# Attention scores of a head across two PSUM banks, one mask-and-maximum instruction per head

## Chip, cores and metric

One core of one Trainium2 chip. The metric is the device time of one execution in microseconds (us); of several runs the median is given. TensorE is PE here, VectorE DVE, ScalarE ACT, GpSimd POOL; SP issues the DMAs.

## What is computed (reference, cut)

One decoder layer on 1024 tokens with 1024 channels, all float32: an input projection, native sparse attention (8 heads of 64, in two groups of 4) beside a gated DeltaNet, an output projection, and a SwiGLU block. The change touches the attention alone. Each query attends three ways, with a softmax of its own each time, and gates mix the results:

```
p_cmp: softmax over 63 compressed keys            (mask: block ends before the query)
idx  : top 8 of 16 blocks of 64 keys by the summed p_cmp (first, own and previous block forced)
o_slc: softmax over the keys of the chosen blocks (causal)
o_win: softmax over the last 512 keys             (causal)
o_nsa = gate0 * o_cmp + gate1 * o_slc + gate2 * o_win
```

## The kernel before

The program is written for a framework that orders each engine's instructions itself, by its own estimates, and sets the semaphores; buffers come from pools with a fixed number per tag. PSUM has 8 banks of 512 float32 per partition.

The attention stage lies between about 470 and 780 us of the span. It walks over 16 units (i, g): i is a block of 128 queries, g a group of 4 heads. For each unit `merge` (L1129) interleaves three generators by weight: `scores` of the next unit, `values` of this one, and as filler `wob` (L1111), the half of the output projection that belongs to the DeltaNet.

`scores` (L917) has two phases of four heads each.

- Local phase. Two matmuls (L941, high and low part of the keys) give the 128 own-block scores and the 64 compressed ones, 192 columns, two heads in one bank; two more (L949) give the up to 512 earlier window scores into another bank. DVE masks the 64 (L942), the earlier window scores (L951) and the own block (L955), and takes the minimum of each piece on the way (an accumulator read follows each such instruction); L955 continues the minimum that L951 found. ACT takes the exponentials (L944, L957) and sums them.
- Then for i of 4 and more the top-8 choice on DVE (L967 to L978), which gives `bm`, one mask value per block of 64 keys.
- Selected phase. The scores of i + 1 blocks of keys (L997) go in pieces of at most 512 into one bank each; DVE masks each piece (L1007, with `bm` for i of 4 and more) and the own block (L1011); ACT takes the exponentials (L1014).
- The reciprocal sums are multiplied by the gates on DVE (L962, L1019), and POOL (DVE for i = 0) scales the probabilities by them (`pscale`, L914).

`values` (L1027) turns the scaled probabilities: pair by pair of 128x128 blocks, four transposes on PE (L1063; L1057 for the compressed ones) into a bank of tag b, a rounded copy on ACT (L1065), the rest on DVE (L1066), and three pairs later the products on PE (L1043) into the one bank of tag c, one for each pair of heads. At the end of a pair of heads ACT copies half of c (L1047) and DVE adds the two halves (L1048).

`wob` adds its 512 columns to the residual through ACT (L1124, out of PSUM) and POOL (L1125).

The banks of the stage: a (scores) 3, b (transposes) 3, c (products) 1, mm (filler) 1.

## Time and profile before

| | |
|---|---|
| median of 3 runs | 1513.57 us (1512.15 to 1517.66) |
| the profiled execution | 1515.43 us, of it span 1513.7 us |
| busy in the span: PE, DVE, ACT, POOL | 1436.1, 964.8, 722.9, 727.1 us |
| attention stage, 480 to 780 us: PE, DVE, ACT, POOL | 284.3, 257.6, 241.3, 169.0 us of 300 |

An engine is busy while any of its instructions runs. On DVE an instruction's duration reaches some 0.07 to 0.08 us past the start of the next one, so the distance of two starts is what it takes of the queue. On PE the ends are modelled, and matmuls overlap: four 128x128 transposes start 0.11 us apart though each lasts 0.27.

### The profile page before, as it was taken

To read this page: it belongs to the slowest core of one execution; us is meant where nothing else is said; L and a number is where in the kernel's file an instruction comes from. 1 tells how busy PE (TensorE), PEld (TensorE's weight loads), DVE (VectorE), ACT (ScalarE), POOL (GpSimd) and SP (SyncE) were. 2 spreads that over 40 slices of the span, in tenths; PEclk is the share of its full clock that TensorE was granted. 3 is DMA by queue.
4 is the path that set the end of the run, shared out by engine and by line. 5 is a ranking of instruction groups with operands and counts; after the bars stand their busy time and mean duration, and the time that the engine had idled before them with its cause. 6 is when DMAs were issued, how large, how long until landed. Compare 5 with 4: busy or idle time off the path is not lost.

```text
span 1513.7 us, 23493 instructions
## 1 busy us (share of the span) xinstructions
PE 1436.1 (95%) x8000; PEld 1225.8 (81%) x8000; DVE 964.8 (64%) x2276; ACT 722.9 (48%) x1604; POOL 727.1 (48%) x763
## 2 busy tenths in 40 slices
PE   8889999989899999999999899999999999999997
PEld 7878877889898787878887688888888887888886
DVE  4326688836635798998956565444444444999955
ACT  5433356236544898788765433323333332344423
POOL 1232235520240665554467666666566663345445
PEclk9999999999998999999999899999999999999998
DMA  8822255487535223101037122222222227544003
GB/s 259 285 65 84 90 184 159 112 189 229 172 108 195 92 74 101 50 22 43 30 124 245 32 88 84 84 84 84 84 84 84 84 84 262 195 135 133 1 1 111
DMA packets 142743, 174.96 MB, mean 116 GB/s; under 512 B 26912, under 2 KB 79392, under 8 KB 142496
## 3 DMA queue, kind: packets, MB, share of 16 engines
q1 hardware_dynamic: 142624, 173.47, 36.6%
q8 instruction: 63, 1.03, 0.3%
q14 instruction: 56, 0.46, 0.1%
HBM read 122.01 MB, written 51.41 MB: 115 GB/s over the span
## 4 chain that ended last, share of the span: by engine, by line
PE 61%; DVE 11%; ACT 5%; issue 4%; POOL 3%; DMA 3%; POOLq 0%; SPq 0%; ACTq 0%; DVEq 0%
PE mm L119 16%; PE mm L121 16%; PE mm L120 16%; PE c L1043 3%; PE b L1063 2%; DVE PT L1066 2%; PE a L610 1%; ACT Ps L1014 1%; DVE cy L429 1%; DMA vT<-gD 1%; PE a L997 1%; PE a L617 1%; ACT PT L1065 1%; DVE tmp L574 1%; PE b L625 1%
## 5 line engine op out<-in xcount | busy, mean ns | idle before, releaser
L1200 POOL TENSOR_TENSOR A<-wq,A 128x512 fp32r<-128x512 f32 x94 | 135.2, 1440 | 87.5 <-ACT A L1199 79.1
L1199 ACT ACTIVATE A<-wq 128x512 fp32r<-128x512 f32 x96 | 60.1, 630 | 133.0 <-PE mm L121 116.9
L119 PE MATMUL mm<-w,xh 128*128 128x256 f32 x384 | 111.7, 291 | 11.7 <-ACT kst L827 6.2
L1066 DVE TENSOR_TENSOR PT<-b,PT 128x512 fp32r<-128x512 f32 (+2 forms) x168 | 103.8, 621 | 19.0 <-ACT PT L1065 17.2
L120 PE MATMUL mm<-w,xh 128*128 128x256 f32 x384 | 110.9, 289 | 1.0 <-POOL w L208 1.0
L121 PE MATMUL mm<-w,xl 128*128 128x256 f32 x384 | 110.6, 288 | 0.0
L1065 ACT ACTIVATE PT<-b 128x512 fp32r<-128x512 f32 (+2 forms) x168 | 89.1, 539 | 37.6 <-PE b L1063 31.2
L1200 POOL TENSOR_TENSOR wk<-wq,wk 128x512 fp32r<-128x512 f32 x61 | 81.5, 1338 | 52.9 <-ACT wk L1199 44.3
L1043 PE MATMUL c<-PT,vs 128*128 128x256 f32 x528 | 92.9, 300 | 0.1
L208 POOL TENSOR_TENSOR w<-wraw,w 128x512 fp32r<-128x512 f32 x48 | 63.4, 1337 | 56.8 <-ACT w L205 56.8
L119 PEld LDWEIGHTS mm<-w,xh 128*128 128x128 f32 x384 | 75.0, 195 | 12.4 <-ACT kst L827 6.4
L1199 ACT ACTIVATE wk<-wq 128x512 fp32r<-128x512 f32 x63 | 39.6, 630 | 87.6 <-PE mm L121 79.9
L119 PE MATMUL mm<-T,A 128*128 128x512 f32 x200 | 79.1, 396 | 0.0
L120 PE MATMUL mm<-T,A 128*128 128x512 f32 x200 | 79.1, 396 | 0.0
L121 PE MATMUL mm<-T,A 128*128 128x512 f32 x200 | 79.1, 396 | 0.0
L120 PEld LDWEIGHTS mm<-w,xh 128*128 128x128 f32 x384 | 75.0, 195 | 1.2 <-POOL w L208 1.2
L119 PE MATMUL mm<-xh,w 128*128 128x512 f32 x192 | 75.6, 394 | 0.0
L121 PE MATMUL mm<-xh,w 128*128 128x512 f32 x192 | 75.2, 392 | 0.0
L121 PEld LDWEIGHTS mm<-w,xl 128*128 128x128 f32 x384 | 74.9, 195 | 0.1
L1043 PEld LDWEIGHTS c<-PT,vs 128*128 128x128 f32 x528 | 73.0, 191 | 2.5 <-DVE PT L1066 0.3
L1501 DVE TENSOR_TENSOR B<-B,mm 128x512 f32<-128x512 f32 x100 | 63.4, 677 | 17.9 <-PE mm L121 15.0
L120 PE MATMUL mm<-xl,w 128*128 128x512 f32 x192 | 74.8, 389 | 0.0
(471 smaller groups left out, 4533.0 us busy)
## 6 DMA issues: line engine op xcount, KB each, us to landing
wq<-in_w_gu SPq DMA_DIRECT2D x92, 256.0 KB, 2.7
aD<-ring SPq DMA_DIRECT2D x44, 256.0 KB, 2.2
ring<-aD SPq DMA_DIRECT2D x44, 256.0 KB, 3.9
raw<-in_w_dn SPq DMA_DIRECT2D x36, 256.0 KB, 3.8
qk<-gD SPq DMA_DIRECT2D x16, 512.0 KB, 4.8
wraw<-in_w_out SPq DMA_DIRECT2D x28, 256.0 KB, 2.9
wraw<-in_w_tok SPq DMA_DIRECT2D x24, 256.0 KB, 3.1
wraw<-in_w_gdn SPq DMA_DIRECT2D x24, 256.0 KB, 2.8
```

Of the source, the lines that this page charges most:

```text
L119: mm(ps, lhsT=lh, rhs=rh, start=first, stop=False, skip_group_check=grow)
L120: mm(ps, lhsT=lh, rhs=rl, start=False, stop=False, skip_group_check=grow)
L121: return mm(ps, lhsT=ll, rhs=rh, start=False, stop=last, skip_group_check=grow)
L208: (lo or G).tensor_tensor(out=wt[:, 1, k0:k0 + n, :], in0=raw, in1=f32(wt[:, 0, k0:k0 + n, :]), op=ALU.subtract)
L429: V.scalar_tensor_tensor(out=y, in0=cr[:, j:j + 512], scalar=cw[:, j:j + 1], in1=y, op0=ALU.mult, op1=ALU.add)
L1043: mm(po[:, 0:256], lhsT=v, rhs=PT[0:K, a, b_ * 256:(b_ + 1) * 256], start=(n_ == 0 and a == 0), stop=(last and b_ == len(vs) - 1 and a == 1))
L1063: tpose(pt[:, o_:o_ + P], src[:, hh, b * P:(b + 1) * P], ident)
L1065: act(out=PT[0:K, 0, 0:w], in_=pt[0:K, 0:w], func=AF.Copy)
L1066: V.tensor_tensor(out=PT[0:K, 1, 0:w], in0=pt[0:K, 0:w], in1=f32(PT[0:K, 0, 0:w]), op=ALU.subtract)
L1199: act(out=dst[:, 0], in_=src, func=AF.Copy)
L1200: after(eng.tensor_tensor(out=dst[:, 1], in0=src, in1=f32(dst[:, 0]), op=ALU.subtract), prev)
L1501: V.tensor_tensor(out=out_, in0=a_, in1=b_, op=op)
```

## The change

- Tag a now has 2 buffers of 1024 columns, two adjacent banks each; b has 2 banks in place of 3; c is one bank that lies allocated throughout, its two halves of 256 columns serving the two pairs of heads; mm stays. That is 4 + 2 + 1 + 1 = 8 banks.
- Local phase: the 192 columns stand at 512 to 703, the earlier window scores end at 511, so the 640 window columns are adjacent over the bank edge. One instruction masks them all (L944 of the changed kernel) from one joint mask `winm`.
- Selected phase: the two pieces lie on either side of the bank edge, and one instruction masks a head's whole row. For i below 4 it uses `winm`; for i of 4 and more it uses `bm` for all blocks, and the causal mask of the own block is added by PE: one more matmul per head (L993), identity by the causal matrix, into the same bank.
- The gates are the second scalar of the scaling, so L962 and L1019 fall away; so does a multiplication in the top-8 choice (L973).
- `wob` adds to the residual on DVE straight from PSUM (L1102); the ACT copy and the POOL addition fall away.

```diff
...
-    add("caus", np.where(c <= r, 0.0, NEG))
-    add("far", np.concatenate([np.where(c > r, 0.0, NEG), np.zeros((P, 384))], 1))
+    add("winm", np.concatenate([np.where(c > r, 0.0, NEG), np.zeros((P, 384)), np.where(c <= r, 0.0, NEG)], 1))
...
+    V.tensor_copy(causr, C("winm")[:, 512:640])
...
     def bank(tag):
-        return mk(pps3, [P, 512], tag, F32, {"mm": 1, "a": 3, "b": 3, "c": 1}[tag])
+        return mk(pps3, [P, 1024 if tag == "a" else 512], tag, F32, {"mm": 1, "a": 2, "b": 2}[tag])
+
+    pvs = mk(pps3, [P, 2, 256], "c", F32)
...
-    def pscale(i, ap, sc, k):
-        (V if i < EARLY[k] else G).tensor_scalar(ap, ap, sc, 1.0, op0=ALU.mult, op1=ALU.mult)
+    def pscale(i, ap, sc, gt, k):
+        (V if i < EARLY[k] else G).tensor_scalar(ap, ap, sc, gt, op0=ALU.mult, op1=ALU.mult)
...
-            if hh == 0:
-                s2 = bank("a")
-            o = hh * 192
+
+            s1 = bank("a")
+            w0_ = 512 - np_ * P
             for a in range(2):
-                mm(s2[:, o:o + 192], lhsT=QS[:, h, :], rhs=KSw[a][:, g, i, :], start=(a == 0), stop=(a == 1))
-            V.tensor_tensor_reduce(out=PC[:, h, 1:65], in0=s2[:, o + P:o + 192], in1=C("cmpm")[:, i * 64:(i + 1) * 64],
+                mm(s1[:, 512:704], lhsT=QS[:, h, :], rhs=KSw[a][:, g, i, :], start=(a == 0), stop=(a == 1))
+            V.tensor_tensor_reduce(out=PC[:, h, 1:65], in0=s1[:, 640:704], in1=C("cmpm")[:, i * 64:(i + 1) * 64],
...
             if np_:
-                s1 = bank("a")
                 for a in range(2):
-                    mm(s1[:, 0:np_ * P].rearrange("p (b t) -> p b t", t=P), lhsT=QS[:, h, :],
+                    mm(s1[:, w0_:512].rearrange("p (b t) -> p b t", t=P), lhsT=QS[:, h, :],
                        rhs=KSw[a][:, g, i - np_:i, 0:P], start=(a == 0), stop=(a == 1))
...
-            V.tensor_tensor_reduce(out=pr[:, np_ * P:nw], in0=s2[:, o:o + P], in1=caus, scale=-0.125, scalar=first,
+            V.tensor_tensor_reduce(out=pr[:, 0:nw], in0=s1[:, w0_:640], in1=winm[:, w0_:640], scale=-0.125, scalar=3e38,
                                    op0=ALU.add, op1=ALU.min, accum_out=mx[:, h, 1:2])
...
-        V.tensor_tensor(out=gr[:, 2, :], in0=gr[:, 2, :], in1=gts[:, 2, :], op=ALU.mult)
...
-            V.tensor_tensor(out=sc[:, 0, :], in0=sc[:, 0, :], in1=C("selm")[:, o16:o16 + 16], op=ALU.mult)
...
-            pscale(i, pr, gr[:, 2, h:h + 1], 0)
+            pscale(i, pr, gr[:, 2, h:h + 1], gts[:, 2, h:h + 1], 0)
...
+            s1 = bank("a")
+
+            n0 = 0 if ns <= 512 else ns // 2
+            o = 512 - n0
+            for (a0, a1) in ((0, n0), (n0, ns)):
+                for a in range(2 if a1 > a0 else 0):
+                    mm(s1[:, o + a0:o + a1], lhsT=QS[:, h, :], rhs=KSs[a][:, g, a0:a1], start=(a == 0),
+                       stop=(a == 1 and (a1 < ns or bm is None)))
+            if bm is None:
+                V.tensor_tensor_reduce(out=pr[:, 0:ns], in0=s1[:, o:o + ns], in1=winm[:, 640 - ns:640], scale=-0.125,
+                                       scalar=3e38, op0=ALU.add, op1=ALU.min, accum_out=mx[:, h, 7:8])
+            else:
+                mm(s1[:, o + i * P:o + ns], lhsT=identr, rhs=causr, start=False, stop=True)
+                V.tensor_tensor_reduce(out=pr[:, 0:ns].rearrange("p (b k) -> p b k", k=64),
+                                       in0=s1[:, o:o + ns].rearrange("p (b k) -> p b k", k=64),
+                                       in1=bc(bm[:, 0:ns // 64].unsqueeze(2), [P, ns // 64, 64]), scale=-0.125,
+                                       scalar=3e38, op0=ALU.add, op1=ALU.min, accum_out=mx[:, h, 7:8])
...
-                V.tensor_tensor(out=gr[:, 1, h2], in0=gr[:, 1, h2], in1=gts[:, 1, h2], op=ALU.mult)
                 for h_ in (h - 1, h):
-                    pscale(i, Ps[hp][:, h_ % 2, 0:ns], gr[:, 1, h_:h_ + 1], 1)
+                    pscale(i, Ps[hp][:, h_ % 2, 0:ns], gr[:, 1, h_:h_ + 1], gts[:, 1, h_:h_ + 1], 1)
...
-                    po.append(bank("c"))
-                po = po[0]
+                po = pvs[:, hp]
...
-        wx = mk(pn, [P, 512], "wx", F32, WXB)
-        act(out=wx, in_=ps, func=AF.Copy)
-        G.tensor_tensor(out=xt, in0=xt, in1=wx, op=ALU.add)
+        V.tensor_tensor(out=xt, in0=xt, in1=ps, op=ALU.add)
```

How it stands in each engine's order. A row names line, operation, output<-inputs and size; numbers belong to buffers; what stands in brackets is the semaphores the instruction waits for. Line numbers are those of the respective kernel: L941/L949 before are L935/L942 now, L942/L951 are L936/L944, L1007 is L994, L1043 is L1022, L1057/L1063 are L1036/L1042, L1066 is L1045.

PE, start of the local phase of block 6, first group. Before:

```order
L941 MATMUL a_7889<-ksw_716_3830,QS_7566 128x192 [waits DVE_49]
L941 MATMUL a_7889<-ksw_717_3831,QS_7566 128x192
L949 MATMUL a_7894<-ksw_716_3830,QS_7566 128x512 [waits DVE_49]
L949 MATMUL a_7894<-ksw_717_3831,QS_7566 128x512
L121 MATMUL mm_7913<-mgt_6980,wo_7906 128x512
L1063 MATMUL b_7917<-cst_75,Pw_7573 128x128 [waits Activation_49,Pool_49]
L1063 MATMUL b_7917<-cst_75,Pw_7573 128x128 [waits Pool_49]
L1063 MATMUL b_7917<-cst_75,Pw_7573 128x128 x2
L949 MATMUL a_7929<-ksw_716_3830,QS_7566 128x512 [waits DVE_49]
L949 MATMUL a_7929<-ksw_717_3831,QS_7566 128x512
```

And now:

```order
L935 MATMUL a_7696<-ksw_717_3832,QS_7395 128x192
L935 MATMUL a_7696<-ksw_718_3833,QS_7395 128x192
L1036 MATMUL b_7705<-cst_75,PC_7400 64x128 [waits DVE_49,Pool_49]
L1036 MATMUL b_7705<-cst_75,PC_7400 64x128
L116 MATMUL mm_7718<-mgt_6851,wo_7711 128x512
L942 MATMUL a_7696<-ksw_717_3832,QS_7395 128x512 [waits DVE_49]
L942 MATMUL a_7696<-ksw_718_3833,QS_7395 128x512
L117 MATMUL mm_7718<-mgt_6851,wo_7711 128x512
L118 MATMUL mm_7718<-mgt_6851,wo_7711 128x512
L1042 MATMUL b_7722<-cst_75,Pw_7402 128x128 [waits Activation_49]
```

The two scores pieces of a head now share a buffer, and the earlier window scores (L942) stand behind other work and wait for DVE. By the count in that wait it is the accumulator read of the same head's L936, the mask of the 64 compressed scores; so it is in all 56 heads that have earlier window scores. Before, the DVE wait of L949 was for a buffer of an earlier head.

DVE, start of the selected phase of block 5, second group, two heads. Before:

```order
L1007 ISA Ps_7753,mx_7570<-a_7754,bm_7698 128x384 [waits DVE_49]
L1007 ISA mx_7570 128x1
L1066 TENSOR_TENSOR PT_7780<-b_7775,PT_7780 128x512 [waits Activation_49]
L1007 ISA Ps_7753,mx_7570<-a_7758,bm_7698,mx_7570 128x256 [waits DVE_49]
L1007 ISA mx_7570 128x1
L1007 ISA Ps_7753,mx_7570<-a_7787,bm_7698 128x384
L1007 ISA mx_7570 128x1
L1011 ISA Ps_7753,mx_7570<-a_7758,cst_16_79,mx_7570 128x128 [waits DVE_49]
L1011 ISA mx_7570 128x1
```

And now, with the addition of `wob` among them:

```order
L994 ISA Ps_7573,mx_7399<-a_7574,bm_7518 128x768 [waits DVE_49]
L994 ISA mx_7399 128x1
L1045 TENSOR_TENSOR PT_7597<-b_7592,PT_7597 128x512 [waits Activation_49]
L994 ISA Ps_7573,mx_7399<-a_7604,bm_7518 128x768 [waits PE_49]
L994 ISA mx_7399 128x1
L1102 TENSOR_TENSOR xt_7423<-xt_7423,mm_7425 128x512 [waits DMAHW4_49,DMAHW3_49,PE_49]
L1045 TENSOR_TENSOR PT_7623<-b_7618,PT_7623 128x512 [waits Activation_49]
```

Three masks with their accumulator reads became one per head; L1102 waits for the last filler matmul and for DMAs.

PE, first products of the second pair of heads, before and now:

```order
L1043 MATMUL c_7772<-PT_7718,vcs_91 128x256 [waits DVE_49]
L1043 MATMUL c_7772<-PT_7718,vcs_91 128x256
L1043 MATMUL c_7772<-PT_7733,vs_5143 128x256 x4
L120 MATMUL mm_7598<-mgt_6980,wo_7591 128x512
L121 MATMUL mm_7598<-mgt_6980,wo_7591 128x512
```

```order
L1042 MATMUL b_7875<-cst_75,Pw_7464 128x128
L1042 MATMUL b_7875<-cst_75,Ps_7630 128x128 [waits Pool_49] x2
L987 MATMUL a_7885<-kss_715_3830,QS_7395 128x448
L1022 MATMUL c_5145<-PT_7831,vcs_92 128x256 [waits DVE_49]
L1022 MATMUL c_5145<-PT_7831,vcs_92 128x256
```

The second pair writes another half of the bank now, and its first product still waits for DVE; by the count it is, in both kernels, the addition of the first pair's halves (L1048, now L1027).

## Rows read from the trace of the kernel before

**Rows 1.** The head of the page: the span, and each engine's busy us, share and instruction count.

```profile
span 1513.7 us, 23493 instructions
PE 1436.1 (95%) x8000; PEld 1225.8 (81%) x8000; DVE 964.8 (64%) x2276; ACT 722.9 (48%) x1604; POOL 727.1 (48%) x763
```

**Rows 2.** The view by stretches: from:to, length, then busy us (instructions) of PE, weight loads, DVE, ACT and POOL, the granted TensorE clock as a share of full speed, the DMA share and GB/s. First the whole attention stage, then parts of it, then what follows.

```profile
480.00:780.00 300.00, 284.27 (x1838) 243.38 (x1838) 257.64 (x1033) 241.27 (x626) 168.96 (x209) 0.98 0.22 72
...
480.00:560.00 80.00, 76.38 (x471) 65.23 (x471) 65.61 (x325) 68.71 (x213) 47.88 (x67) 0.93 0.34 113
640.00:700.00 60.00, 56.10 (x377) 47.98 (x377) 54.98 (x209) 50.16 (x124) 32.87 (x39) 1.00 0.10 35
778.00:1513.00 735.00, 715.25 (x3193) 583.26 (x3191) 438.64 (x630) 263.34 (x454) 413.38 (x304) 0.98 0.32 104
```

**Rows 3.** The view of waits, 480 to 780 us, for PE's weight loads: engine, line <- what it waited for, us in total, times, longest.

```profile
PEld c L1043 <- DVE mn L1048: 8.3, 12, 1.6
PEld a L941 <- DVE mx L955: 4.8, 11, 0.9
PEld mm L119 <- DMA mgt<-mgD: 2.5, 1, 2.5
...
PEld a L949 <- DVE mx L955: 1.7, 2, 1.5
...
PEld a L949 <- DVE mx L951: 1.1, 3, 0.5
```

**Rows 4.** The view by lines with shapes kept apart, 480 to 780 us: DVE's masks and what the change touches (busy us, mean ns | idle before).

```profile
L955 DVE CUSTOM_DVE_ANT_0 Pw<-a,cst,mx 128x128 f32<-128x128 f32 x56 | 19.3, 344 | 0.4
L1011 DVE CUSTOM_DVE_ANT_0 Ps<-a,cst,mx 128x128 f32<-128x128 f32 x56 | 18.8, 342 | 0.3
...
L951 DVE CUSTOM_DVE_ANT_0 Pw<-a,cst 128x512 f32<-128x512 f32 x32 | 21.9, 683 | 1.0 <-PE a L949 0.9
L951 DVE CUSTOM_DVE_ANT_0 Pw<-a,cst 128x384 f32<-128x384 f32 x8 | 4.4, 555 | 0.3
...
L1019 DVE TENSOR_TENSOR gr<-gr,gate 128x2 f32<-128x2 f32 x30 | 6.7, 224 | 0.2
L962 DVE TENSOR_TENSOR gr<-gr,gate 128x4 f32<-128x4 f32 x15 | 3.6, 237 | 0.1
L973 DVE TENSOR_TENSOR sc<-sc,cst 128x16 f32<-128x16 f32 x8 | 2.7, 338 | 0.0
...
L1172 DVE TENSOR_TENSOR ring<-xt,mm 128x512 f32<-128x512 f32 x2 | 1.4, 686 | 3.1 <-PE mm L121 3.1
```

**Rows 5.** The same view with shapes together, 460 to 790 us: the second pieces of the selected scores, and their accumulator reads (of all pieces).

```profile
L1007 DVE CUSTOM_DVE_ANT_1 Ps<-a,bm,mx 128x192 f32<-128x192 f32 (+3 forms) x32 | 16.3, 510 | 1.1
...
L1007 DVE DVE_READ_ACCUMULATOR2_ANT mx<- 128x1 f32 x88 | 7.1, 80 | 0.0
```

**Rows 6.** DVE's timeline at 643 and 651 us: start, duration, line.

```profile
643.61 0.15 DVE L1019 TENSOR_TENSOR gr<-gr,gate 128x2 f32<-128x2 f32 x1
643.68 0.74 DVE L1100 SCALAR_TENSOR_TENSOR mn<-mn,vec,b 128x512 f32<-128x512 f32 x1
...
651.18 0.34 DVE L955 CUSTOM_DVE_ANT_0 Pw<-a,cst,mx 128x128 f32<-128x128 f32 x1
651.45 0.08 DVE L955 DVE_READ_ACCUMULATOR2_ANT mx<- 128x1 f32 x1
651.45 0.68 DVE L951 CUSTOM_DVE_ANT_0 Pw<-a,cst 128x512 f32<-128x512 f32 x1
```

**Rows 7.** PE's timeline at 640 us: the nearest to the added matmul, 128 columns against the identity.

```profile
640.52 0.54 PE L871 MATMUL b<-identr,qh 128*128 128x128 f32 x4
```

**Rows 8.** Timeline at 646 to 651 us, PE, DVE and ACT: a first scores piece and its mask, then one bank of transposes from PE over ACT to DVE, and the PE instruction that waits for that bank.

```profile
646.53 0.45 PE L941 MATMUL a<-ksw,QS 128*128 128x192 f32 x2
...
647.02 0.23 DVE L942 CUSTOM_DVE_ANT_0 PC<-a,cst 128x64 f32<-128x64 f32 x1
647.17 0.08 DVE L942 DVE_READ_ACCUMULATOR2_ANT mx<- 128x1 f32 x1
...
648.01 0.60 PE L1063 MATMUL b<-cst,Ps 128*128 128x128 f32 x4
...
649.96 0.58 ACT L1065 ACTIVATE PT<-b 128x512 fp32r<-128x512 f32 x1
...
650.29 0.38 PE L1063 MATMUL b<-cst,Ps 128*128 128x128 f32 x2
...
650.58 0.69 DVE L1066 TENSOR_TENSOR PT<-b,PT 128x512 fp32r<-128x512 f32 x1 [0.70 <-ACT PT L1065]
...
651.32 0.30 PE L1057 MATMUL b<-cst,PC 128*64 128x128 f32 x1 [0.17 <-DVE PT L1066]
```

**Rows 9.** Waits of ACT and costs on POOL, 480 to 780 us: the addition of `wob`, and the scaling.

```profile
ACT wx L1124 <- PE mm L121: 9.2, 8, 2.7
...
L915 POOL TENSOR_SCALAR Ps<-Ps,gr 128x256 f32<-128x256 f32 (+6 forms) x56 | 44.2, 805 | 25.1 <-DVE gr L1019 13.7 <-PE mm L121 5.7 <-ACT wx L1078 2.9
L915 POOL TENSOR_SCALAR Pw<-Pw,gr 128x640 f32<-128x640 f32 (+3 forms) x56 | 38.7, 713 | 0.7
...
L1125 POOL TENSOR_TENSOR xt<-xt,wx 128x512 f32<-128x512 f32 x16 | 20.7, 1296 | 17.9 <-ACT wx L1124 17.8
```

More of the change, by code (lines that the diff above doesn't have):

```diff
@@ L59, in _constants @@
     s = np.arange(16)[None, :]
-    ms, as_ = [], []
+    as_ = []
     for i in range(4, NT):
@@ L63, in _constants @@
         forced = (s == 0) | (s == cur) | (s == cur - 1)
-        ms.append(np.where(forced | (s > cur), 0.0, 1.0))
         as_.append(np.where(forced, BIG, np.where(s > cur, NEG, 0.0)))
-    add("selm", np.concatenate(ms, 1))
     add("sela", np.concatenate(as_, 1))
@@ L176, in hybrid_block @@
     identr = mk(pcr, [P, P], "identr", F32R)
+    causr = mk(pcr, [P, P], "causr", F32R)
     ones = mk(pc, [P, P], "ones")
@@ L902, in hybrid_block @@
         dma(f32(VS[:, i]).rearrange("p h d -> p (h d)"), vD[i])
-    def slc_pieces(i):
-        n = P * (i + 1)
-        k = -(-n // 512)
-        return [(j * n // k, (j + 1) * n // k) for j in range(k)]
-    caus = C("caus")
-    far = C("far")
+    winm = C("winm")
     EARLY = (1, 1, 0)
-    def pscale(i, ap, sc, k):
-        (V if i < EARLY[k] else G).tensor_scalar(ap, ap, sc, 1.0, op0=ALU.mult, op1=ALU.mult)
+    def pscale(i, ap, sc, gt, k):
+        (V if i < EARLY[k] else G).tensor_scalar(ap, ap, sc, gt, op0=ALU.mult, op1=ALU.mult)
     def scores(u):
@@ L992, in scores @@
             pr = Ps[hp][:, hh]
-            first = 3e38
-            for (a0, a1) in slc_pieces(i):
-                s1 = bank("a")
-                for a in range(2):
-                    mm(s1[:, 0:a1 - a0], lhsT=QS[:, h, :], rhs=KSs[a][:, g, a0:a1], start=(a == 0), stop=(a == 1))
-                e = min(a1, i * P)
-                if e > a0:
-                    if bm is None:
-                        msk = far[:, P:P + e - a0]
-                        o_, i_ = pr[:, a0:e], s1[:, 0:e - a0]
-                    else:
-                        msk = bc(bm[:, a0 // 64:e // 64].unsqueeze(2), [P, (e - a0) // 64, 64])
-                        o_ = pr[:, a0:e].rearrange("p (b k) -> p b k", k=64)
-                        i_ = s1[:, 0:e - a0].rearrange("p (b k) -> p b k", k=64)
-                    V.tensor_tensor_reduce(out=o_, in0=i_, in1=msk, scale=-0.125, scalar=first, op0=ALU.add,
-                                           op1=ALU.min, accum_out=mx[:, h, 3 + a0 // 256:4 + a0 // 256])
-                    first = mx[:, h, 3 + a0 // 256:4 + a0 // 256]
-                if a1 == ns:
-                    V.tensor_tensor_reduce(out=pr[:, i * P:ns], in0=s1[:, i * P - a0:ns - a0], in1=caus,
-                                           scale=-0.125, scalar=first, op0=ALU.add, op1=ALU.min,
-                                           accum_out=mx[:, h, 7:8])
@@ L1034, in values, with products @@
             pairs = [None] + [blk[b:b + 2] for b in range(0, len(blk), 2)]
-            po = []
-            def products(hp, n_, K, vs, PT, po, last):
-                if n_ == 0:
-                    po.append(bank("c"))
-                po = po[0]
+            def products(hp, n_, K, vs, PT, last):
+                po = pvs[:, hp]
                 for b_, v in enumerate(vs):
                     for a in range(2):
-                        mm(po[:, 0:256], lhsT=v, rhs=PT[0:K, a, b_ * 256:(b_ + 1) * 256],
+                        mm(po, lhsT=v, rhs=PT[0:K, a, b_ * 256:(b_ + 1) * 256],
                            start=(n_ == 0 and a == 0), stop=(last and b_ == len(vs) - 1 and a == 1))
@@ L1046, in products @@
                     tmp = mk(pn, [64, 256], "otmp", F32, 2)
-                    act(out=tmp, in_=po[64:128, 0:256], func=AF.Copy)
+                    act(out=tmp, in_=po[64:128], func=AF.Copy)
                     V.tensor_tensor(out=mn[hp * 64:(hp + 1) * 64, g * 2:g * 2 + 2, i * P:(i + 1) * P],
-                                    in0=po[0:64, 0:256].rearrange("p (h t) -> p h t", h=2),
+                                    in0=po[0:64].rearrange("p (h t) -> p h t", h=2),
                                     in1=tmp.rearrange("p (h t) -> p h t", h=2), op=ALU.add)
@@ L1066, in values @@
                 V.tensor_tensor(out=PT[0:K, 1, 0:w], in0=pt[0:K, 0:w], in1=f32(PT[0:K, 0, 0:w]), op=ALU.subtract)
-                todo.append((products, (hp, n_, K, vs, PT, po, n_ == len(pairs) - 1)))
+                todo.append((products, (hp, n_, K, vs, PT, n_ == len(pairs) - 1)))
                 if len(todo) > LAG:
```

6 lines of the change are left out of this document (removed).

## The prediction

> **What bounds the kernel now.** I read the page's head first [rows 1]. PE is busy 95% of the span and DVE 64%, so over the whole kernel nothing on DVE should count. But the change touches one stage only, and the view by stretches [rows 2] shows that stage apart: from 480 to 780 us PE has 284.3 of 300 us, DVE 257.6 (86%), ACT 241.3 (80%), POOL 169.0 (56%); from 640 to 700 DVE is at 55.0 of 60 (92%). What follows (778 to 1513) has 715.3 of 735 on PE and stays as it is. The granted clock is 0.98 in the stage, the upper level of 2.4 GHz for nearly all of it, and only the beginning is lower (0.93 from 480 to 560).
>
> So two engines are nearly full, and each waits for the other. The waits of PE's weight loads [rows 3] name the traffic: 8.3 us in 12 waits for DVE's addition of the c halves, 4.8 and 1.7 for L955, 1.1 for L951. These four, 15.9 us, all end on DVE. They are a lower bound of what PE loses to DVE, since a matmul row that lasts until the next one starts hides a stall. PE is the bound by its busy share; DVE is the engine that ends its waits. A shorter DVE queue can therefore pay, but only up to what PE really waits.
>
> **DVE, what goes.** For each of 56 heads L955 with its accumulator read falls away and the mask next to it grows by 128 columns; L1011 does the same in the selected phase (24 of its 56 where the head had one piece, 32 where it had two), and 32 second pieces of L1007 are joined to the first. A mask costs 683 ns for 512 columns and 555 for 384 [rows 4], so 1.0 ns a column and about 171 fixed. The timeline [rows 6] shows what an instruction takes of the queue: 651.18 to 651.45, 0.27 us, for an L955 whose duration is 344 ns. Its read starts together with the next mask, so a read hides, though it has a row of 80 ns [rows 5]. Joining 128 columns to a neighbour saves 0.27 − 0.13 = 0.14 us. That happens 80 times (56 L955, 24 L1011): 11.2 us. In the 32 heads from i = 4 on, L1011 goes wholly to the widened row (0.14) and the second piece's fixed start goes too (0.14): 0.28 × 32 = 9.0. The small operations, 32 L1019, 16 L962 and 8 L973, have 224, 237 and 338 ns [rows 4], but L1019 takes 643.61 to 643.68 of the queue [rows 6]; with the longer ones I take 0.1 each: 5.6. Together 25.8 us.
>
> **DVE, what comes.** 16 additions of `wob` out of PSUM, 512 columns: the like of L1172, 686 ns [rows 4], less the 0.07 that overlap, 0.61 × 16 = 9.8. Net, the DVE queue is shorter by **16 us**. By durations alone it would be 56 × (0.344 − 0.128) + 24 × (0.342 − 0.128) + 32 × (0.342 + 0.510 − 0.128 − 0.21) + 12 of small ones + 144 reads × 0.08 − 11, some 45: that counts overlap twice, and is the upper end.
>
> **ACT and POOL.** ACT loses 16 copies of some 0.6 us (the like of the 0.58 of L1065 [rows 8]), POOL 16 × 1.296 = 20.7 us [rows 9]. Neither is the bound: POOL has 131 us free in the stage. I take nothing. The scaling with two scalars by pointer has no row; L915 has one pointer and takes 44.2 + 38.7 = 82.9 us in all [rows 9]. If a second pointer cost nothing that stays; if each scaling cost per column what the two-tensor addition does (1296 ns for 512, where L915's long form has about half), it doubles, and POOL stands at 169 − 20.7 + 83 = 231 of 300. I take 0, since L915 is the nearest instruction; what covers it either way is POOL's free time, but in the upper case the scaled rows come later to PE's transposes by up to 0.8 us a row.
>
> **PE, what comes.** 32 matmuls of identity by the causal matrix. The nearest row [rows 7] has four of 128 columns in 0.54 us from the first's start to the last's end. If a single one lasts about 0.25, an estimate, the starts lie (0.54 − 0.25) / 3 = 0.097 apart: **+3.1 us** for 32. The upper end is 0.25 each, 8.0.
>
> **The new wait.** The earlier window scores (L942 now) stand in the same buffer as the 192 columns, and wait for the accumulator read of the mask of the 64 compressed scores (L936 now, L942 in the rows). In the trace [rows 8] such a pair starts at 646.53 and lasts 0.45, its mask starts at 647.02 and the read ends at 647.25: some 0.6 us behind the second matmul's start. PE fills that with what the order puts between, by the rows of the change `wob` matmuls or transposes; a bank of transposes is 0.60 us [rows 8]. Counting these through the 56 heads, an estimate, the filler is 0.8 us in the mean and too short in 24 heads, by 3.1 us in all when DVE is free at once. If a subtraction of 0.69 us [rows 8] stands ahead of L936 on DVE, 45 heads come short, by 25 us. I take **+3.1** and keep 25 for the range. What queues behind a waiting L942 on PE is everything: transposes, products and filler.
>
> A rule speaks against this part. The Trainium skill (PSUM — Partial Sum Buffer, PSUM bank collisions raise a hardware error) wants PSUM guarded by bank and 32-partition quadrant, not by address. The 192 columns and the window scores lie in different banks of the buffer, so by that rule L942 need not wait at all and the sum would be 3.1 us lower; the program waits by buffer. No run here shows it yet.
>
> **Two b banks for three.** A bank of transposes is held from 648.01 until the subtraction ends at 651.27 [rows 8], 3.26 us, of which 1.35 pass between the end of the transposes (648.61) and ACT's start (649.96). With two banks the pair at 650.29 would have waited until 651.27, 1.0 us. If that happened once in each of 16 units it were 16 us; if the shorter DVE queue shortens the hold, nothing. I take **+1**, nearest to the lower end, since PE had other work to go on with at 650.29 and the waits [rows 3] name no b bank; 16 is kept for the range.
>
> **The halves of c.** The second pair of heads now has its own half, which should take away part of the 8.3 us [rows 3]. But by the order its first product still waits for the addition of the first pair's halves. I take 0, between 0 and −8.3.
>
> **The addition of `wob` on DVE.** ACT waited 9.2 us for its matmuls in 8 waits [rows 9]. That wait is now DVE's, and behind it stand the subtractions (L1045) that release b banks. Where DVE stands at L1102, PE is computing filler, so PE is not idle meanwhile, but the next products are late. Between 0 and 9.2 I take **+1**: most of such waiting is for a PE that works, and cost nothing on ACT.
>
> **Sum.** −16 + 3.1 + 3.1 + 1 + 1 = −7.8 us. The −16 passes to PE in full only because PE's waits on DVE are 15.9 at the least [rows 3] and DVE, at 92% in the middle of the stage, sets the pace there. The profiled execution took 1515.4, so 1507.6; the median lies 1.9 lower, hence **1506** (1505.7).
>
> **The rivals.**
>
> *Full relief.* DVE is the bound of the whole stage and its durations count: the queue is 45 shorter, of which PE takes back its named 15.9 and about as much again that its rows hide, some 28, less 4 to 8 for what PE gets to do: −20 to −24, 1490 to 1494, with 1486 if the c halves help too. For it: DVE at 92% and PE's waits ending on it. Against: PE at 95%, and the overlaps of [rows 6].
>
> *No relief.* PE is the bound; matmul rows hide little stall, DVE's waits just end elsewhere. Then 0 to +7 remain (the 7.2 of the new terms, with at most as much relief): 1513 to 1521. For it: 284.3 of 300 on PE.
>
> *The local phase in lock-step, slower.* In each head PE must now give L935, DVE must mask, and only then can PE give L942, after which DVE waits for PE: one round trip of two engines a head, where before both pairs of matmuls ran ahead into three buffers. With only two transposes banks there is less filler to put between. Price: 25 us if a subtraction stands ahead of L936 in every head, 17 if in two of three; with 3 for the identity, 4 for b (1.0 us in one unit of four) and 4 to 16 of the 16 still gained, 17 + 3 + 4 − 12 = **+12** (8 to 20), 1526 (1522 to 1534). It decides from the point at which a DVE instruction of 0.6 us or more stands ahead of L936 in two heads of three; at 92% that is likely in the middle of the stage and not at 82% (65.6 of 80) of the beginning [rows 2].
> The Trainium skill (Perfetto Trace Analysis, Matmuls) says that independent matmul groups should rotate through different PSUM banks, so that the evacuation of one overlaps the next group. By it, fewer buffers for scores (three to two) and transposes (three to two) cost time; the trace of before shows no wait for b among PE's largest, so it doesn't bear the rule out yet.
>
> *The change doesn't do what it says.* The c halves serve nothing, as above; this is within the forecast.
>
> **How the numbers follow.** About 0.5%, 7.6 us, is what a measurement here can tell from no change. The forecast's case, −1 to −15, has 0.52; its middle is at that bound, so 0.27 of it is faster and 0.25 the same. Full relief has 0.12, faster. No relief 0.13, the same. Lock-step 0.23, slower. Faster 0.39, same 0.38, slower 0.23. The range must reach into both outer cases: from 1492, which leaves out some 0.08 of full relief, to 1524, which leaves out about 0.12 of lock-step. The forecast's own range is 1499 to 1513.
>
> **What would show it.** Right: DVE's busy time from 480 to 780 falls by 16 to 45 us with one mask per head and none of L955, L1011, L962, L1019; the stage is some 8 us shorter; PE's waits for DVE's masks shrink; POOL falls by about 20. Wrong: waits of PE's L942 on the L936 mask (PC or its minimum) of over 10 us, or of L1042 for a DVE subtraction; DVE waiting for PE at L1102 or L944; the stage no shorter while DVE's busy share falls below 80%, which would mean that PE alone was the bound; a scaling row on POOL well above 805 ns.

## The result and the profile after

The changed kernel takes 1524.84 us (median of 5 runs, 1519.79 to 1527.75), before 1513.57: the ratio is 1.0057, 95% interval 1.0038 to 1.0076. A second set of 9 runs, shown below, gave 1.0052 (1.0032 to 1.0071). The prediction was 1506, range 1492 to 1524: the wrong side, and just outside the range. The profiled execution is the slowest of the five, 1527.75 us.

The page's head, to be laid beside [rows 1]:

```profile
span 1525.9 us, 23231 instructions
...
PE 1453.3 (95%) x8032; PEld 1235.6 (81%) x8032; DVE 944.0 (62%) x1949; ACT 718.1 (47%) x1588; POOL 719.2 (47%) x747
```

The view by stretches, columns as in [rows 2]:

```profile
470.00:496.00 26.00, 24.13 (x89) 18.68 (x89) 16.54 (x88) 17.49 (x70) 5.69 (x7) 0.54 0.69 242
...
480.00:780.00 300.00, 284.22 (x1799) 239.37 (x1798) 230.25 (x690) 227.63 (x586) 148.96 (x185) 0.96 0.20 63
...
640.00:700.00 60.00, 56.15 (x379) 48.41 (x378) 50.02 (x133) 47.81 (x115) 33.11 (x38) 1.00 0.13 41
```

DVE is busy for 230.3 us in place of 257.6, 83% in place of 92% from 640 to 700, and PE is as full as before, 284.2. But the stage is longer now, so the same 300 us hold less of it. From the stage's first score to the start of its last product, the view by stretches of before and of after says:

```profile
470.48:793.01 322.53, 303.11 (x1953) 259.24 (x1952) 271.04 (x1094) 253.69 (x668) 172.96 (x213) 0.97 0.24 80
```

```profile
468.38:803.03 334.65, 317.69 (x1983) 266.89 (x1984) 251.19 (x765) 248.69 (x651) 161.84 (x197) 0.95 0.24 77
```

So the change took 19.8 us from DVE (20.8 by the pages' heads), 5.0 from ACT and 11.1 from POOL, whose scaling became slower (below). DVE is far less busy and nothing is gained: that is a case the prediction named as wrong, though its reading of it, that PE alone is the bound, is not what the runs below show.

Where the time went, from PE's timelines of both. Before, first the stage's first score, then the first score of unit 3 (block 1, second group) and of unit 15 (the last), and what follows the last product:

```profile
470.48 0.47 PE L941 MATMUL a<-ksw,QS 128*128 128x192 f32 x3
...
502.42 0.41 PE L941 MATMUL a<-ksw,QS 128*128 128x192 f32 x2
...
734.74 0.36 PE L941 MATMUL a<-ksw,QS 128*128 128x192 f32 x2
...
793.13 0.40 PE L119 MATMUL mm<-ms,wo 128*128 128x512 f32 x1
```

After, the same places (the last row holds the last six products; the last one starts at 793.0 before and at 803.0 now):

```profile
468.38 0.44 PE L935 MATMUL a<-ksw,QS 128*128 128x192 f32 x2 [1.18 <-DVE vst L819]
...
502.94 0.32 PE L935 MATMUL a<-ksw,QS 128*128 128x192 f32 x1
...
742.33 0.36 PE L935 MATMUL a<-ksw,QS 128*128 128x192 f32 x2
...
802.44 0.87 PE L1022 MATMUL c<-PT,vs 128*128 128x256 f32 x6
```

| us | before | after | after, second trace |
|---|---|---|---|
| up to the first score | 470.5 | 468.4 | 466.4 |
| units 0 to 2 | 31.9 | 34.6 | 34.0 |
| units 3 to 14 | 232.3 | 239.4 | 237.3 |
| unit 15 to the last product | 58.3 | 60.7 | 59.8 |
| the rest | 720.7 | 722.9 | 721.8 |

Units 3 to 14 lost 5 to 7 us, nearly all at the upper level of the clock (0.99 in this stretch, 1.00 in the second trace): some 2 us are the identity products (the work in the table below), the rest is waiting. The first three units lost 2 to 3 at the lower level: from 470 to 496 the granted clock is 0.54 with PE 93% busy (24.13 of 26), where before it was 0.74 with PE at 21.67. In the changed kernel PE stands idle for 1.18 us ahead of the first score, and the clock falls soon after. All twelve traces of the changed kernel and its variants have this idle time, and 17 to 24 us at the lower level between 465 and 500 us (after_w 10); the eight of the kernel before and its variants have no such idle time, and 10 to 14 us. Which part of the change moved this, no run settles. Over the whole execution the clock is not what costs the time: it averages 0.978 in the 14 runs of the changed kernel as in 129 of before, and among the runs between 0.979 and 0.981 the medians are 1521.2 (4 runs) and 1513.0 (57). The time up to the first score differs between the traces although the matmuls there are the same, in the same order; why stays open.

PE's waits, columns as in [rows 3], 480 to 780 us:

```profile
PEld a L942 <- DVE mx L936: 9.6, 25, 0.8
PEld b L1042 <- PE a L935: 4.8, 10, 0.7
PEld c L1022 <- DVE mn L1027: 4.0, 10, 1.2
PEld c L1022 <- ACT PT L1044: 3.8, 8, 1.2
PEld b L1042 <- DVE PT L1045: 3.6, 9, 0.7
```

Of the waits for L955 and L951 in [rows 3], 7.6 us, 0.9 are left (for L944), and the wait for the c halves fell from 8.3 to 4.0. In their place: 9.6 us in 25 waits of the window scores for the mask of the compressed ones, and waits of the transposes (L1042), which had none of that size before. DVE's own waits, same stretch, show who is late now:

```profile
DVE PT L1045 <- ACT PT L1044: 27.0, 49, 1.6
DVE Pw L944 <- PE a L942: 12.1, 17, 2.8
...
DVE xt L1102 <- PE mm L118: 5.3, 1, 5.3
```

Before, the first of these was 13.3 us in 30. The last is a single wait, at 489 us, for the filler's first sum; the prediction named it, and first_wobold below, which doesn't have it, is no faster. DVE stands waiting at the links of the chain, not behind a queue. One local phase in the timeline of PE and DVE (ACT's and the rest left out):

```profile
672.22 0.45 PE L935 MATMUL a<-ksw,QS 128*128 128x192 f32 x2
672.35 0.08 DVE L944 DVE_READ_ACCUMULATOR2_ANT mx<- 128x1 f32 x1
672.35 0.41 DVE L1045 TENSOR_TENSOR PT<-b,PT 64x256 fp32r<-64x256 f32 x1
672.71 0.23 DVE L936 CUSTOM_DVE_ANT_0 PC<-a,cst 128x64 f32<-128x64 f32 x1
...
672.91 0.63 PE L1042 MATMUL b<-cst,Pw 128*128 128x128 f32 x4 [0.24 <-DVE PT L1045]
673.29 0.71 PE L942 MATMUL a<-ksw,QS 128*128 128x512 f32 x2
673.84 0.36 PE L935 MATMUL a<-ksw,QS 128*128 128x192 f32 x2
673.91 0.69 DVE L1045 TENSOR_TENSOR PT<-b,PT 128x512 fp32r<-128x512 f32 x1 [0.97 <-ACT PT L1044]
674.52 0.81 DVE L944 CUSTOM_DVE_ANT_0 Pw<-a,cst 128x640 f32<-128x640 f32 x1
```

L942 starts 1.07 us behind its L935 (672.22 to 673.29): the mask of the compressed scores stands behind a subtraction on DVE and starts at 672.71, and the transposes in between wait for a bank themselves. DVE then has nothing to do for 0.97 us until ACT's copy comes, and only at 674.52 gets to the mask of the window.

### The profile page after: what moved, and what is told of

Its sections match the earlier page's. It is cut to its first block, busy times and chain, and to the rows that moved or that the text cites. A ratio compares the mean times of both kernels' runs of the same rounds, so it can differ in the third digit from the quotient of the medians.

```text
span 1525.9 us, 23231 instructions
## 1 busy us (share of the span) xinstructions
PE 1453.3 (95%) x8032; PEld 1235.6 (81%) x8032; DVE 944.0 (62%) x1949; ACT 718.1 (47%) x1588; POOL 719.2 (47%) x747
## 4 chain that ended last, share of the span: by engine, by line
PE 64%; DVE 8%; ACT 4%; issue 4%; POOL 4%; DMA 3%; DVEq 0%; ACTq 0%; POOLq 0%; SPq 0%
PE mm L116 16%; PE mm L117 16%; PE mm L118 16%; PE c L1022 4%; PE b L1042 3%; DVE PT L1045 1%; PE a L987 1%; PE a L609 1%; ACT PT L1044 1%; DVE cy L428 1%; DMA vT<-gD 1%; PE a L616 1%; PE a L942 1%; PE b L624 1%; ACT Pw L946 1%
## 5 line engine op out<-in xcount | busy, mean ns | idle before, releaser
L1045 DVE TENSOR_TENSOR PT<-b,PT 128x512 fp32r<-128x512 f32 (+2 forms) x168 | 104.0, 621 | 34.6 <-ACT PT L1044 33.2
L1177 POOL TENSOR_TENSOR wk<-wq,wk 128x512 fp32r<-128x512 f32 x61 | 82.5, 1353 | 52.5 <-ACT wk L1176 44.1
L1022 PE MATMUL c<-PT,vs 128*128 128x256 f32 x528 | 94.3, 301 | 0.0
L1022 PEld LDWEIGHTS c<-PT,vs 128*128 128x128 f32 x528 | 73.8, 192 | 3.1 <-issue 0.4
```

The lines of the kernel that those rows point to most:

```text
L1022: mm(po, lhsT=v, rhs=PT[0:K, a, b_ * 256:(b_ + 1) * 256], start=(n_ == 0 and a == 0), stop=(last and b_ == len(vs) - 1 and a == 1))
L1045: V.tensor_tensor(out=PT[0:K, 1, 0:w], in0=pt[0:K, 0:w], in1=f32(PT[0:K, 0, 0:w]), op=ALU.subtract)
L1177: after(eng.tensor_tensor(out=dst[:, 1], in0=src, in1=f32(dst[:, 0]), op=ALU.subtract), prev)
```

## Experiments

All ratios are to the kernel before on the same chip, in 5 rounds. Each has an interval of 0.12 to 0.22% to either side, so a difference of two is known to some 3 to 4 us. To compare variants, PE's time from unit 3 to unit 14 is taken apart: the distance from one matmul's start to the next, against the 20th percentile of that distance for the same tile and shape of the earlier one, over the kernels compared. The sum of the percentiles is called work, the excess stall, and it is booked to the matmul that came late. Some 15 us of the transposes' stall (14.7 to 17.6) lie between two transposes in a row, in every kernel.

| kernel | ratio (interval) | units 3–14 | work | stall | local scores | transposes | products | filler |
|---|---|---|---|---|---|---|---|---|
| before | 1 | 232.3 | 179.4 | 52.9 | 12.0 | 17.8 | 15.3 | 5.1 |
| changed | 1.0057 (1.0038–1.0076) | 239.4 | 181.4 | 58.0 | 12.7 | 27.2 | 12.6 | 2.9 |
| changed, again | 1.0052 (1.0032–1.0071) | 237.3 | 181.4 | 55.9 | 12.4 | 26.2 | 12.4 | 2.4 |
| b2 | 0.9996 (0.9984–1.0007) | 232.1 | 180.3 | 51.8 | 7.4 | 26.9 | 11.7 | 3.5 |
| gates | 0.9982 (0.9967–0.9996) | 230.9 | 179.4 | 51.5 | 10.6 | 17.1 | 16.1 | 4.9 |
| ident | 1.0009 (0.9993–1.0025) | 236.5 | 181.4 | 55.1 | 12.7 | 17.2 | 18.6 | 4.2 |
| ident_zero | 1.0056 (1.0035–1.0076) | 238.9 | 181.4 | 57.4 | 12.6 | 18.0 | 18.9 | 4.5 |
| noident | 1.0026 (1.0011–1.0041) | 233.7 | 179.8 | 53.9 | 12.7 | 26.7 | 11.0 | 1.6 |
| first | 1.0016 (0.9997–1.0035) | 234.0 | 181.4 | 52.5 | 3.5 | 30.0 | 12.4 | 4.5 |
| first_noident | 1.0000 (0.9985–1.0015) | 231.9 | 179.8 | 52.2 | 3.6 | 30.4 | 12.1 | 3.6 |
| first_dve | 1.0088 (1.0067–1.0108) | 240.0 | 181.4 | 58.6 | 3.7 | 34.0 | 13.3 | 4.9 |
| before_dve | 1.0055 (1.0033–1.0077) | 245.7 | 183.7 | 62.0 | 17.7 | 21.7 | 14.4 | 3.1 |

In the changed kernel the stall at the local scores is hardly more than before (12.7 and 12.0): the new wait took the place of the old ones. What rose is the transposes' stall, by 9.4.

**The two new prices, taken out one by one.** The window scores ahead of the mask (first), that is

```diff
+            if np_:
+                for a in range(2):
+                    mm(s1[:, w0_:512]...)          # moved up from below
             V.tensor_tensor_reduce(out=PC[:, h, 1:65], in0=s1[:, 640:704], ...)
```

> The changed kernel, with a head's earlier window scores issued ahead of the mask of its compressed scores, so that PE no longer waits for DVE between the two. Theory 2 (lock-step in the local phase): 4 to 10 us faster than the changed kernel, with its 9.6 us of PE waiting for that mask gone. Theory 1 (transposes banks): within 2 us of the changed kernel, the waits turning up at the transposes.

1.0057 or 1.0052 became 1.0016: about 6 us (4 between the two kernels without the products, below). The lock-step's wait is gone, the local scores' stall falls from 12.7 to 3.5, and the waits of the transposes took over part of it (first, 480 to 780 us):

```profile
PEld b L1042 <- DVE PT L1045: 9.5, 22, 1.2
PEld c L1022 <- DVE mn L1027: 5.2, 11, 1.3
```

Without the identity product (noident; it leaves out the mask, so it computes something else):

```diff
-                mm(s1[:, o + i * P:o + ns], lhsT=identr, rhs=causr, start=False, stop=True)
```

> The changed kernel without the 32 products of identity and causal mask; the own block of the selected scores is thus not masked for i of 4 and more. 32 x 0.06 (the distance that these matmuls keep in the trace) = 1.9 us faster than the changed kernel by the work alone. If the added matmuls also delay the masks behind them: 3 to 5 us faster.

4 to 5 us, more than the work. In the timeline the next matmul starts 0.06 us behind such a product, so 32 of them are 1.9 us; the table's work differs by 1.6, for the 28 of them in units 3 to 14. The rest is order and waits. Both at once:

> Both edits at once: the changed kernel with the window scores ahead of the mask and without the products of identity and causal mask (the own block of the selected scores is thus not masked for i of 4 and more). If the two prices are separate (5.8 and 4.6 us of the 8.6): 2 us faster than before. If each edit mostly rearranged the order and its waits: no better than each alone, 1515 to 1518.

1.0000: 2.4 us better than first and 3.9 better than noident, less than the 4 to 6 that each edit gave to the changed kernel, so the prices overlap; and even without both, the kernel is only as fast as before (2.3 us to either side). The shorter DVE queue bought nothing there that these runs can tell.

**The pieces on the kernel before.** Two banks for the transposes:

```diff
-        ..., {"mm": 1, "a": 3, "b": 3, "c": 1}[tag])
+        ..., {"mm": 1, "a": 3, "b": 2, "c": 1}[tag])
```

> The kernel before, with two banks for the transposes instead of three, and nothing else. Theory 1 (the gain of the change was spent on new waits, and the lost third bank is one of them): 5 to 10 us slower than before, with waits of the transposes for DVE's subtraction that were 0.5 us before now at 4 us or more. Theory 2 (the new waits are those of the earlier window scores for the mask of the compressed ones; the bank is not missed): within 2 us of before. Theory 3 (PE's clock falls more often, whatever the waits): within 2 us at the same time spent at the lower clock.

No loss in the ratio. The transposes wait (before it was 0.5 us in this view for L1063; b2, 480 to 780 us),

```profile
PEld b L1063 <- DVE PT L1066: 5.3, 16, 0.9
...
PEld a L941 <- DVE mx L955: 1.3, 4, 0.5
```

and the wait that [rows 3] showed at L941 shrinks from 4.8 to 1.3: in the table 9.1 us more at the transposes, 4.6, 3.6 and 1.6 less elsewhere. PE is held back once, and it matters little at which instruction. A small price may hide behind the clock: these runs were granted 0.981 in the mean, and at the same clock (0.979 to 0.981) their median is 1515.4 (8 runs) against before's 1513.0.

Gates in the scaling, without L962, L1019 and L973:

```diff
-        (V if i < EARLY[k] else G).tensor_scalar(ap, ap, sc, 1.0, ...)
+        (V if i < EARLY[k] else G).tensor_scalar(ap, ap, sc, gt, ...)
-        V.tensor_tensor(out=gr[:, 2, :], in0=gr[:, 2, :], in1=gts[:, 2, :], op=ALU.mult)
...
```

> The kernel before, with only the gates folded into the scaling and the multiplication of the top-8 choice left out: 56 small instructions fewer on DVE, 5.6 us of its queue by the prediction's count, nothing added anywhere. If DVE sets the pace of the stage: 3 to 6 us faster than before. If PE's own work sets it: within 2 us. If the scaling with two pointers costs POOL time, its rows stand above 805 and 713 ns.

DVE 251.7 in place of 257.6 (from first score to last product 263.8 in place of 271.0), and 0.9982. Once more:

> The kernel before with the gates in the scaling, once more, beside the other run on the same chip. 56 small DVE instructions fewer; at 0.3 us of time per us of DVE busy (some 13 us of durations, 5.6 of its queue) 2 to 4 us faster: 0.997 to 0.999, as the first time (0.9982). If the first was luck: 0.999 to 1.001.

0.9996 (0.9980 to 1.0013). Between 0.6 and 2.7 us for some 7 us of DVE; no change lies outside the first interval and inside the second.

The causal mask on PE (32 products more, 32 masks fewer), and 32 products of zeros with all masks kept:

```diff
+                if a1 == ns and bm is not None:
+                    mm(s1[:, i * P - a0:ns - a0], lhsT=identr, rhs=causr, start=False, stop=True)
-                e = min(a1, i * P)
+                e = min(a1, i * P) if bm is None else a1      # not in ident_zero
```

> The kernel before with the causal mask of the selected scores added by PE for i of 4 and more: 32 masks of 128 columns fewer on DVE (4.5 us of its queue by the prediction's count), 32 products more on PE (1.9 us by their distance in the trace). If a product costs what leaving them out gave back (4.6 us): 2 to 5 us slower than before. If DVE's relief reaches PE: 1 to 3 us faster. If both are small: within 1.5 us.

> The kernel before with 32 products of identity by a matrix of zeros into the selected scores, and all its masks as they were: the price of the products alone. By their distance in the trace 1.9 us; if the price is that of the run in which they took over the mask (2 to 4 us slower) or more, the 32 masks that fell away there gave nothing or little back; the difference of the two is what 32 masks fewer on DVE are worth.

The products alone cost 0.56%, against 1.9 us of work. With the masks that they replace left out, most of it comes back (0.47%, 7 us, give or take 4); that the masks are worth so much is not shown, since by the pages' heads they are 4.2 us of DVE (969.2 to 965.0). Both differences hold some luck of the order: the same instructions with a slightly altered weight (before_w and after_w),

```diff
-        return [0.5 + 0.13 * n] * 4 + [3.0 if i >= 4 else 0.6] + ...
+        return [0.55 + 0.13 * n] * 4 + [3.1 if i >= 4 else 0.65] + ...
```

> The kernel before with the weight of a unit's scores in the interleaving raised by some 3 to 8% (0.5 to 0.55, 3.0 to 3.1, 0.6 to 0.65): the same instructions in a slightly different order. This measures how much the order alone does: if the differences of 2 to 5 us between the variants are mostly such order, this kernel is 2 to 5 us off as well; if they belong to the edits, it is within 1.5 us of before.

> The changed kernel with the same altered weights. If 7.9 us over before is the price of the edits: within 2 us of the changed kernel. If a good part is the order that this planner happened to find: 3 us or more off, to either side.

came out at 1.0024 (1.0005 to 1.0042) and 1.0087 (1.0069 to 1.0106), 3.6 and 5 us slower than with the old weights (part of the 3.6 is a lower clock: between 0.979 and 0.981 the median of before_w is 1514.8, against 1513.0). So a single difference of under some 5 us between two of these kernels is no proof of its edit. I rest on those that are larger or show in two pairs: the lock-step (6 and 4 us), the products (4 to 5, 2.4 and 8.5), DVE's load (10.9 and 8.3).

**What a DVE us is worth.** An addition of 128 columns behind each head's mask of a block from 1 on, to no purpose:

```diff
+            if i:
+                V.tensor_tensor(out=scr, in0=winm[:, 0:128], in1=bc(mx[:, h, 1:2], [P, 128]), op=ALU.add)
```

> The changed kernel with the window scores ahead of the mask, and with 112 additions of 128 columns more on DVE, one behind each head's mask, into a scratch buffer that nobody reads: some 0.2 us each, 20 to 25 us of its queue, so that DVE has about as much to do as before the change. If the shorter DVE queue is worth nothing to PE: within 2 us of the kernel without them. If it is worth what the prediction took, and something else ate it: 10 us or more slower.

> The kernel before with the same 112 additions on DVE: its queue in the stage goes from 258 to some 280 of 300 us. If DVE set the pace before the change, as the prediction took it: 15 us or more slower. If PE's and ACT's chain did: under 8 us. The slope beside that of the other run tells how the worth of a DVE us depends on how full DVE is.

The pages' heads of first, first_dve and before_dve, to be laid beside [rows 1]:

```profile
PE 1445.6 (95%) x8032; PEld 1229.5 (81%) x8032; DVE 945.7 (62%) x1949; ACT 717.8 (47%) x1588; POOL 718.8 (47%) x747
```

```profile
PE 1448.2 (95%) x8032; PEld 1231.4 (81%) x8032; DVE 979.7 (64%) x2061; ACT 718.2 (47%) x1588; POOL 721.0 (47%) x747
```

```profile
PE 1446.0 (95%) x8000; PEld 1229.4 (81%) x8000; DVE 996.6 (65%) x2388; ACT 724.7 (47%) x1604; POOL 729.9 (48%) x763
```

The stretch of the stage, first_dve, then before_dve:

```profile
480.00:780.00 300.00, 279.82 (x1794) 235.97 (x1794) 265.21 (x791) 226.33 (x580) 152.38 (x186) 0.97 0.19 61
```

```profile
480.00:780.00 300.00, 279.79 (x1788) 235.25 (x1788) 288.46 (x1140) 237.75 (x615) 160.14 (x200) 0.98 0.20 66
```

DVE is 34.0 us busier than in first and 31.8 than before; the time rises by 1.0088 − 1.0016 = 0.72%, 10.9 us, and by 0.55%, 8.3 us. That is 0.32 and 0.26 us for each us of DVE (0.16 to 0.44 with the intervals), and no steeper with DVE at 96% of the stretch than at 88%. In before_dve 2.5 us of filler more fell into units 3 to 14. The same load on ACT:

```diff
+            if i:
+                act(out=scr, in_=bc(mx[:, h, 1:2], [P, 128]), func=AF.Copy)
```

> The same with the 112 operations of 128 columns on ACT instead of DVE, some 0.2 to 0.3 us each, 20 to 30 us. If ACT is now the engine whose work PE ends up waiting for (DVE waits 29 us for its copies in the changed kernel): 10 us or more slower, and more than with the additions on DVE. If neither engine's load counts, only the order: within 3 us.

1.0042 (1.0028 to 1.0056), 3.9 us for 17.7 us more of ACT (735.5 against 717.8 by the pages' heads): 0.2. Neither DVE nor ACT sets the pace alone.

**What didn't help.** All of these have the window scores ahead of the mask. The addition of `wob` back on ACT and POOL:

```diff
-        V.tensor_tensor(out=xt, in0=xt, in1=ps, op=ALU.add)
+        act(out=wx, in_=ps, func=AF.Copy)
+        G.tensor_tensor(out=xt, in0=xt, in1=wx, op=ALU.add)
```

> The changed kernel with the window scores ahead of the mask and with the addition of wob on ACT and POOL, as it was. DVE loses 16 additions, 9.8 us of its queue. If PE's waits for the subtractions (8.7 us with the window scores ahead) come from a full DVE queue: 3 to 6 us faster than with the window scores ahead alone. If they come from the number of banks: within 2 us of it.

1.0014 (0.9999 to 1.0029), as first. Products four pairs behind:

```diff
-    LAG = 3
+    LAG = 4
```

> The changed kernel with the window scores ahead of the mask, and the products four pairs behind their transposes in place of three, with five buffers for the turned probabilities. If PE's waits are latency of the chain from transposes over ACT and DVE to the products: 3 to 6 us faster than without. If the two transposes banks set the wait: within 2 us.

1.0006 (0.9993 to 1.0018): 1.5 us, within the luck of an order. Three banks shared by transposes and filler:

```diff
+        tag = "b" if tag == "mm" else tag
-        ..., {"mm": 1, "a": 2, "b": 2}[tag])
+        ..., {"a": 2, "b": 3}[tag])
```

> The changed kernel with the window scores ahead of the mask, and with three banks that the transposes and the filler share in place of two and one. With the window scores ahead, PE waits 10.4 us for the subtraction that frees a transposes bank. If the lost bank is where the gain went: 4 to 8 us faster than with the window scores ahead alone, that is 3 to 6 us faster than before. If the filler holds the third bank most of the time, or the waits move elsewhere as they did in the kernel before with two banks: within 2 us.

1.0057 (1.0036 to 1.0077): slower. In its trace units 3 to 14 are 1.1 us shorter than those of first and the first three 1.0 longer; from unit 15 on it takes 3.1 us more, at a granted clock of 0.95 where first has 1.00. A third bank for the transposes alone has no room beside the four of the scores and was not tried. The put-together version:

```diff
-                mm(s1[:, o + i * P:o + ns], lhsT=identr, rhs=causr, start=False, stop=True)
...
+                V.tensor_tensor_reduce(out=pr[:, nb:ns], in0=s1[:, o + nb:o + ns], in1=winm[:, 512:640], scale=-0.125,
+                                       scalar=mx[:, h, 3:4], ..., accum_out=mx[:, h, 7:8])      # nb = i * P
```

> What the runs point to, put together: the changed kernel with the window scores ahead of the mask, the products four pairs behind, and the causal mask of the own block back on DVE for i of 4 and more, in place of the identity product. Without the products 3 to 5 us less than the run with the products four pairs behind (1.0006); 32 more masks on DVE at some 0.3 us of time per us of DVE, 2 to 3 us more. If both prices hold: 0.998 to 1.000 of before; if the masks cost as much as the products: 1.000 to 1.002.

1.0028 (1.0010 to 1.0046): a miss. It has masks in place of the products and is 3.3 us slower than first_lag, within the luck of an order.

**The repeat of the changed kernel:**

> The changed kernel once more, for runs beside those of its variants and for a second trace. If the 1.0057 was an unlucky draw: 1.002 to 1.004. If it holds: 1.005 to 1.007, with the stage again some 14 us longer than before's and the time ahead of the stage again some 3 us shorter.

1.0052: it holds. The stage is 331.2 us from its first score to its last product (797.6 − 466.4), 8.7 longer than before's 322.5; in the first trace it was 334.6.

## Why the prediction was wrong, point by point

**The step that failed is "The −16 passes to PE in full", from waits of 15.9 us and a DVE at 92%.** The queue did get shorter, by 20.8 us of busy time over the execution (within the 16 to 45 named), but a DVE us added cost 0.26 to 0.32 us; at that price 20.8 taken away are worth 5 to 7, and where the new prices are out (first_noident) nothing of it is seen. What took the 5 to 7 stays open; they are of the size of an order's luck. The named waits showed who came last, not what would follow. A bank of transposes suggests why. From PE's first transpose to the end of DVE's subtraction, by their rows in the timelines from 540 to 745 us (115 banks before, 111 after, means): before, 0.60 transposes, 0.62 waiting for ACT, 0.55 ACT's copy, 0.43 waiting for DVE, 0.63 subtraction, 2.83 us; in the changed kernel 0.63, 0.45, 0.54, 0.27, 0.63, that is 2.53. All that a free DVE could take from this chain is 0.43 us; 1.8 is work of three engines one after the other. Even the 0.16 less of waiting for DVE need not be the shorter queue: b2, two banks and DVE as busy as before, has 0.27 there as well, and 2.58 in all. By an estimate from these means, with two banks and one started every 1.8 us, 2.5 leaves PE 1 us of slack a pair, and in bursts none.

**The new wait was taken at 3.1 us and is worth 4 to 6** (first). The upper end of 25 was far off. The Trainium skill's rule (PSUM — Partial Sum Buffer, PSUM bank collisions raise a hardware error), to guard PSUM by bank and quadrant, was not put to use by any run: in first the program still waits by buffer, and the mask of the compressed scores starts after the window scores in all 56 heads. What first shows is the price of the wait, up to twice the 3.1.

**The identity products were taken at 3.1 (8.0 at most).** By themselves they are 1.9; left out they gave back 2.4 to 5, and zeros on the kernel before cost 8.5, of which some 4 to 5 can be order. What exceeds 1.9 is no matmul time but stall; in ident_zero it stands at the products of `values` (15.3 to 18.9 us in the table). Why there, no run settles.

**Two b banks at +1:** b2 gave 0.9996, −2.4 to +1.1 us, where +1 was taken from 0 to 16. Right in size on the kernel before. In the changed kernel the transposes' stall is 9 us more and the relief of DVE is missing by about as much; that the third bank would give it back was not shown. The Trainium skill's rule on rotating through banks (Perfetto Trace Analysis, Matmuls) holds for the waits, 5.3 us where there were 0.5; in the time b2's ratio shows no price.

**The halves of c at 0:** the wait fell from 8.3 to 4.0, but in b2, with the old halves, it fell to 3.3 as well. It moved with the order. **`wob` on DVE at +1:** not contradicted, first_wobold is 0.3 us from first, give or take 4. **The scaling at no cost:** POOL's rows rose by a tenth (below), 9.2 us in all, covered as said (gates has the same rows and is no slower than before). That is why POOL fell by 11 us and not by the 20 that were named.

**The rivals.** The lock-step was the slower one, +12 (8 to 20) with 17 us for the wait. It came as +8 to +9, with 4 to 6 for the wait, 2 to 5 for the identity products, and no relief in place of 12 us of it. Mechanism right, its terms not: a DVE instruction of 0.6 us or more ran when the second matmul of a head's 192 scores ended, or started ahead of L936, in 31 of 56 heads, near the two in three of its condition, yet PE waited in only 25, by 0.8 us at most and 9.6 in all. "No relief", at 0.13 and same, was the half of the result that mattered; the two were kept apart as rivals where they came together, so the range ended 0.84 us short of the first five runs.

## What to carry to other kernels

Where several in-order engines pass a tile along and none is idle, a busy share of 90% is no proof of a bound: add a known load to the engine and read the slope before counting on relief from it. The waits name the last in line, and when one goes, the next takes its place (b2: 9 us moved, no loss in the ratio). Compare a stage that got longer or shorter from its first to its last instruction, not over the same microseconds: here that makes 19.8 us of 27.4. Putting two results into one buffer saves instructions and ties their writers to their readers: issue all writers of a buffer ahead of its first reader.

## What the runs showed of the hardware

A second pointer scalar in place of a constant makes POOL's scaling slower by a tenth in the mean, and by about the same 0.07 to 0.09 us at every width (484 to 553 ns for 256 columns, 1129 to 1206 for 1024); gates, which changes little else, has 878 and 784 ns. POOL's rows of the changed kernel, against 805 and 713 ns in [rows 9]:

```profile
L910 POOL TENSOR_SCALAR Ps<-Ps,gr,gate 128x256 f32<-128x256 f32 (+6 forms) x56 | 48.7, 881 | 28.5 <-DVE gr L1002 28.3
L910 POOL TENSOR_SCALAR Pw<-Pw,gr,gate 128x640 f32<-128x640 f32 (+3 forms) x56 | 43.4, 791 | 14.3 <-DVE gr L950 14.3
```

A 128-column product with the identity has a row of 0.23 us and holds up the next matmul by 0.06:

```profile
735.39 0.23 PE L993 MATMUL a<-causr,identr 128*128 128x128 f32 x1
735.45 0.61 PE L1042 MATMUL b<-cst,Ps 128*128 128x128 f32 x4
```

A mask over the bank edge costs what its columns cost and nothing for the edge. DVE, 480 to 780 us, against 683 ns for 512 columns in one bank in [rows 4]: 512 columns over the edge take 685, and 640 take (819 − 683) / 128 = 1.06 ns more a column:

```profile
L944 DVE CUSTOM_DVE_ANT_0 Pw<-a,cst 128x640 f32<-128x640 f32 x32 | 26.1, 819 | 8.6 <-PE a L942 8.4
...
L944 DVE CUSTOM_DVE_ANT_0 Pw<-a,cst 128x512 f32<-128x512 f32 x8 | 5.5, 685 | 0.9 <-PE a L942 0.7
```
